# Projection weights split once: both parts kept in DRAM and reloaded as one piece for blocks 1 to 3

## The chip, the core and the metric

The kernel runs on one core of a Trainium2 chip. The metric is device microseconds of one execution. The engines named below are TensorE (matmuls; PE in the profile, its weight loads PEld), VectorE (DVE), ScalarE (ACT), GpSimd (POOL) and SyncE (SP), whose queue issues nearly all DMAs.

## The reference

A decoder layer over 2048 tokens of width 1024, all in float32:

```
h    = rmsnorm(x)
proj = h @ w_in                                   # 1024 x 3840
o    = concat(hgrn2(proj[:, :2048]), rwkv7(proj[:, 2048:]))     # two recurrences, 512 columns each
x    = x + o @ w_out                              # 1024 x 1024
x    = x + conv_ffn(rmsnorm(x))                   # up 1024 -> 2*2816, conv of width 3, SiLU gate, down
out  = rmsnorm(x)
```

## The kernel before

A product of two float32 matrices is made of three matmuls: each operand is split into a high part, its value in the type fp32r, and a low part, the rest. `mm3` (L286 to L288) multiplies high by high, high by low and low by high and sums them in PSUM. The split itself is a cast on ScalarE (L238 or L245) and a subtraction on VectorE (L239 or L246); `split` also takes the two buffers for the parts.

Phase 1 goes over four blocks of 512 tokens. `dense` is a list of jobs for TensorE: "A" transposes the normalized rows of a block into `hh` and `hl`, 30 jobs "P" multiply 128 columns of w_in each (8 steps of `mm3`, 24 matmuls), and "O", `out_block`, multiplies the finished output of the recurrences with w_out and adds x. An out_block has two halves of 256 tokens, `i2`; each half goes over two halves of the columns, `dh`, with 8 steps of k; each step loads one piece of w_out (128x512), splits it and multiplies it with two groups of 128 tokens, six matmuls. So the same 16 pieces of w_out are loaded and split twice per block. Jobs O of blocks 0 and 1 stand before the jobs of blocks 2 and 3, and that of block 2 at the end. Of w_in, `load` takes a job's weights as two halves of 128x4x128, and a job's load is called one job ahead (`load(i + 1)`), also across an O. The two recurrences (`rw_super`, `hg_unit`) advance in turn, and `fill` lets the dense jobs run between their stages for a fixed credit of estimated time (`TICK`).

Phase 2 begins with block 3's output projection (`o_operand`, `o_weights`), whose w_out pieces go through a ring of four raw slots, then comes the feed-forward part.

Instructions are not issued in the order of the code: the framework's scheduler simulates the kernel with costs of its own and a priority by program order, puts each engine's instructions in the order in which they start there, and gives out the buffers of a pool's tag as they come free. A tile waits for a free buffer of its tag. The tags here are "wraw" (4 buffers of 2 KB per partition, for raw weights, and also for x rows `xh` and the norms' scratch `nsq`), "wh" and "wl" (4 buffers each). The names with numbers below are tiles and their versions; `cst`, `gdt`, `g2`, `rw` and `yo` belong to the RWKV7 stream, `pj` is a PSUM bank of the dense jobs, `oT` is the recurrences' output in DRAM and `x1d` the residual there. ScalarE's functions come in sets, and changing the set is an instruction of its own, ACT_TABLE_LOAD: L114 where the code asks for it, L118 where it is put in ahead of an activation of another set.

Of the kernel before, what the change touches and what calls it, by code (L numbers as in the profile page):

```python
# [7 lines left out]
F32 = mybir.dt.float32  # L8
F32R = mybir.dt.float32r
# [9 lines left out]
P = 128  # L19
T = 2048  # L20
D = 1024
KD = D // P
# [38 lines left out]
def tile_layer(ctx, tc, consts, x, norm1_w, w_in, hg_lb_logits, hg_norm_w, rw_shift_mu, rw_w0, rw_w2,  # L61
# [3 lines left out]
    nc = tc.nc  # L65
    V, S, TE = nc.vector, nc.scalar, nc.tensor
    dma = nc.sync.dma_start

    cp = ctx.enter_context(tc.tile_pool(name="cp", bufs=1, reuse_waits="tile"))
    dp = ctx.enter_context(tc.tile_pool(name="dp", bufs=1, space=DRAM))  # L70
# [101 lines left out]
    KH = NFF // 2  # L172
    Sg = [[dp.tile([KH * P, BLK], F32, name=f"Sg{g}{i}") for i in range(4)] for g in range(2)]
    Tw = [dp.tile([KH * P, BLK], F32, name=f"Tw{i}") for i in range(4)]

    def krows(t_, q, kk):

        return t_[(q * KH + kk) * P:(q * KH + kk + 1) * P, :]
# [58 lines left out]
    def split_to(hi, lo, src):  # L237
        S.copy(hi, src)  # L238
        V.tensor_sub(lo, src, hi.bitcast(F32))  # L239

    def split(pool, src, shape, name, bufs):

        hi = pool.tile(shape, F32R, tag=name + "h", name=name + "h", bufs=bufs)
        lo = pool.tile(shape, F32R, tag=name + "l", name=name + "l", bufs=bufs)
        S.copy(hi, src)  # L245
        V.tensor_sub(lo, src, hi.bitcast(F32))  # L246
        return hi, lo
# [10 lines left out]
    def square_sum(junk, src, b, i, dh):  # L258

        q = 2 * ((b - 2) * 4 + i) + dh  # L260
        act(junk, src, AF.Square, accum_out=ssc[:, q:q + 1])
# [22 lines left out]
    def mm3(acc, lhs, rhs, first, last, skip=False):  # L284
        (lh, ll), (rh, rl) = lhs, rhs
        TE.matmul(acc, lh, rh, start=first, stop=False, skip_group_check=skip)  # L286
        TE.matmul(acc, lh, rl, start=False, stop=False, skip_group_check=skip)  # L287
        TE.matmul(acc, ll, rh, start=False, stop=last, skip_group_check=skip)  # L288

    def phase1(c1):  # L290
        hp = c1.enter_context(tc.tile_pool(name="hp", bufs=1, reuse_waits="tile"))
        wp = c1.enter_context(tc.tile_pool(name="wp", bufs=2, reuse_waits="tile"))
# [22 lines left out]
        def bank(kind):  # L315
            return ps.tile([P, 512], F32, tag=kind, name=kind, bufs=2)
# [79 lines left out]
        def out_block(nb, oh=None, ol=None):  # L396


            def half(t_, k):

                return t_[:, 4 + k // 2, (k % 2) * 256:(k % 2) * 256 + 256]

            for i2 in range(2):
                for dh in range(2):
                    accs = [bank("pj") for _ in range(2)]
                    for k in range(KD):
                        if i2 == 0 and dh == 0 and oh is None:
                            raw = wp.tile([P, BLK], F32, tag="wraw", name="oraw", bufs=4)
                            dma(raw, oT[nb][k * P:(k + 1) * P, :])
                            split_to(hh[:, k, :], hl[:, k, :], raw)  # L410
                        if i2 == 0 and dh == 1 and oh is not None:
                            raw = wp.tile([P, 256], F32, tag="wraw", name="oraw", bufs=4)
                            dma(raw, oT[nb][k * P:(k + 1) * P, 256:512])
                            split_to(half(hh, k), half(hl, k), raw)
                        raw = wp.tile([P, 512], F32, tag="wraw", name="woraw", bufs=4)
                        dma(raw, w_out[0, k * P:(k + 1) * P, dh * 512:dh * 512 + 512])
                        wh, wl = split(wp, raw, [P, 512], "w", 4)
                        if k == KD - 2:
                            xh = [wp.tile([P, 512], F32, tag="wraw", name="xh", bufs=4) for _ in range(2)]
                            for q in range(2):  # L420
                                t0 = nb * BLK + (i2 * 2 + q) * P
                                dma(xh[q], x[0, t0:t0 + P, dh * 512:dh * 512 + 512])
                        for q in range(2):
                            is_ = slice((i2 * 2 + q) * P, (i2 * 2 + q + 1) * P)
                            if oh is None:
                                lhs = hh[:, k, is_], hl[:, k, is_]
                            elif i2 == 0:
                                lhs = oh[k // 4][:, k % 4, is_], ol[k // 4][:, k % 4, is_]
                            else:
                                lhs = tuple(half(t_, k)[:, q * P:(q + 1) * P] for t_ in (hh, hl))  # L430
                            mm3(accs[q], lhs, (wh, wl), k == 0, k == KD - 1)
                            yield 680
                    for q in range(2):
                        V.tensor_add(xh[q], accs[q], xh[q])
                        r0 = (i2 * 2 + q) * P
                        if nb == 2:
                            square_sum(wp.tile([P, 512], BF16, tag="wraw", name="nsq", bufs=4), xh[q], 2,
                                       i2 * 2 + q, dh)
                        dma(x1d[nb][r0:r0 + P, dh * 512:dh * 512 + 512], xh[q])
# [51 lines left out]
        def dense():  # L491
# [39 lines left out]
            cols = [jb[1] for jb in jobs if jb[0] == "P"]  # L531
            loaded = {}

            def load(i):
                if i < len(cols) and i not in loaded:
                    ws = []
                    for k2 in range(2):
                        raw = wp.tile([P, 4, P], F32, tag="wraw", name="wraw", bufs=4)
                        dma(raw, w_in[0, k2 * 512:k2 * 512 + 512, cols[i]:cols[i] + P].rearrange("(k p) c -> p k c", p=P))
                        ws.append(split(wp, raw, [P, 4, P], "w", 4))  # L540
                    loaded[i] = ws

            i = 0
            load(0)
            for jb in jobs:
                if jb[0] == "E":
# [8 lines left out]
                if jb[0] in "OW":  # L555
                    while done["rw2"] < 2 * jb[1] + 2 or done["hg"] < 4 * jb[1] + 4:
                        yield None
                    if jb[0] == "W":
                        jb[2]()
                    else:  # L560
                        yield from out_block(jb[1], *(rows["O"] if jb[1] == 2 else ()))
                    continue
                _, col, ev, cond, fin = jb
                while not cond():
                    yield None
                load(i)
                ws = loaded.pop(i)
                load(i + 1)
                i += 1
                acc = bank("pj")  # L570
                for k in range(KD):
                    wh, wl = ws[k // 4]
# [491 lines left out]
    with ExitStack() as c2:  # L1064
# [6 lines left out]
        Bh, Bl = ([B_[f"{c}{i}"] for i in range(7)] for c in "hl")  # L1071
# [49 lines left out]
        for i, (lo_, hi_) in enumerate(((0, 88), (88, 176))):  # L1121
            vps = pst("cps")
            TE.transpose(vps[:, 0:88], crow[i], ident[0:88, 0:88])
            V.tensor_copy(cvt[:, lo_:hi_], vps[:, 0:88])
        rings = {"o": (Bh[2], []), "w": (Bl[2], [])}

        def ring(nm, src):

            t_, n_ = rings[nm]
            v = t_[:, len(n_) % 4, :]  # L1130
            n_.append(0)
            dma(v, src)
            return v
# [7 lines left out]
        def o_weights(k, dh):  # L1141

            wh, wl = (wr.tile([P, 512], F32R, tag="uraw", name="wo" + c, bufs=6) for c in "hl")
            split_to(wh, wl, ring("w", w_out[0, k * P:(k + 1) * P, dh * 512:dh * 512 + 512]))
            return wh, wl

        junk = uc.tile([P, 512], BF16, tag="c", name="nsq", bufs=6)
# [4 lines left out]
        for n, k in enumerate(ks):  # L1152
            op = o_operand(k)
            if n == 3:
                A0 = up_raw(0, A0_)
            if n in (4, 6):
                for i in range(4):
                    dma(xh_[2 * n - 8 + i], x[0, 3 * BLK + i * P:3 * BLK + (i + 1) * P, (n // 2 - 2) * BLK:(n // 2 - 1) * BLK])
            for dh in range(2):
                w = o_weights(k, dh)  # L1160
                for i in range(4):
                    is_ = slice(i * P, (i + 1) * P)
                    mm3(accs[dh][i], (op[0][:, is_], op[1][:, is_]), w, n == 0, n == KD - 1)
                if n == KD - 1:
                    for i in range(4):
                        xt = xh_[4 * dh + i]
                        V.tensor_add(xt, accs[dh][i], xt)
                        square_sum(junk, xt, 3, i, dh)
                        dma(x1d[3][i * P:(i + 1) * P, dh * BLK:(dh + 1) * BLK], xt)
            if n >= 2:  # L1170
                for q in range(2 * n - 4, 2 * n - 2):
                    build(0, (0, 1, 4)[q // 4], q % 4)
# [167 lines left out]
    with tc.tile_pool(name="dn", bufs=1, reuse_waits="tile") as dn:  # L1340
# [59 lines left out]
        for s_ in range(3, N):  # L1400
            g, p, kk = steps[s_]
# [53 lines left out]
```

## Time and profile before

| | |
|---|---|
| runs | 2796.88 us median of 3 (2792.88 to 2805.77) |
| profiled execution | 2796.34 us, span 2794.2 us |
| mean granted TensorE clock | 0.985 |
| HBM read / written | 325.94 MB / 105.91 MB |
| input projections of blocks 0, 1, 2, 3 | about 0-330, 330-560, 720-950, 1080-1330 us |
| output projections of blocks 0, 1, 2 | about 560-720, 950-1080, 1330-1450 us |
| phase 2 | from about 1450 us |

In the rows of stretches each engine stands with its busy time and its instructions, in the order PE, PEld, DVE, ACT, POOL, and then the granted clock (1.00 is full), the mean busy share of the 16 DMA queues and GB/s. In rows of groups "out<-in" are tile names, then partitions x elements and type, then the count, the busy us and mean ns of one, and the idle time of the engine ahead of them with what ended it.

### The profile page before, as it was taken

How to read it: one execution, taken by the hardware profiler on the slowest of the kernel's cores; microseconds unless marked ns; L12 is line 12 of the kernel's file. 1: busy time of each engine (PE TensorE's matmuls, PEld its weight loads, DVE VectorE, ACT ScalarE, POOL GpSimd, SP SyncE). 2: the span in 40 equal slices, each digit the busy share in tenths (PEclk: the TensorE clock that was granted, in tenths of full speed). 3: DMA queues.
4: the chain of work that ended last, by engine and by line, in shares of the span. 5: the costliest groups of instructions: out<-in, count | busy, mean ns of one | idle time of the engine just before them, and what ended most of it. 6: DMA issues, size and time to landing. Idle time of an engine off the chain costs nothing.

```text
span 2794.2 us, 47708 instructions
## 1 busy us (share of the span) xinstructions
PE 2681.3 (96%) x18059; PEld 2133.3 (76%) x18059; DVE 2061.9 (74%) x3875; ACT 1408.5 (50%) x2236; POOL 4.0 (0%) x10
## 2 busy tenths in 40 slices
PE   6999999989999989999889999999999999999998
PEld 5777778766787767777768887887888888777887
DVE  4877768694586855777748889978989877667656
ACT  4545454543645424735446555556555555445444
POOL 0000000000000000000000000000000000000000
PEclk9999999998999989999899999999999999999999
DMA  4222323244352345542357767525455423999865
GB/s 151 72 71 73 101 69 82 62 140 124 95 153 64 92 130 158 158 129 84 99 186 274 232 215 257 186 73 181 154 200 189 132 79 128 326 326 319 286 193 186
DMA packets 429204, 435.01 MB, mean 156 GB/s; under 512 B 68279, under 2 KB 287661, under 8 KB 428973
## 3 DMA queue, kind: packets, MB, share of 16 engines
q1 hardware_dynamic: 428077, 429.33, 48.3%
q8 instruction: 142, 2.33, 0.3%
q0 software_dynamic: 608, 2.10, 0.2%
q14 instruction: 89, 0.73, 0.1%
q10 hardware_dynamic: 288, 0.52, 0.0%
HBM read 325.94 MB, written 105.91 MB: 155 GB/s over the span
## 4 chain that ended last, share of the span: by engine, by line
PE 39%; DMA 5%; DVE 5%; issue 2%; ACT 1%; SPq 1%; DVEq 0%; ACTq 0%
PE ua L286 5%; PE ua L288 5%; PE ua L287 5%; PE ud L288 2%; PE ud L286 2%; PE ud L287 2%; PE db L287 2%; PE db L286 2%; PE db L288 2%; PE da L287 2%; PE da L288 1%; PE da L286 1%; PE ub L288 1%; PE ub L286 1%; PE ub L287 1%
## 5 line engine op out<-in xcount | busy, mean ns | idle before, releaser
L286 PE MATMUL pj<-hh,wh 128*128 128x512 f32 x960 | 400.9, 418 | 4.4 <-DVE hl L482 4.4
L287 PE MATMUL pj<-hl,wh 128*128 128x512 f32 x960 | 380.4, 396 | 0.0
L288 PE MATMUL pj<-hh,wl 128*128 128x512 f32 x960 | 379.2, 395 | 0.0
L245 ACT CAST wh<-wraw 128x512 fp32r<-128x512 f32 x240 | 147.3, 619 | 339.0 <-PE pj L287 273.6
L286 PE MATMUL ua<-Bh,uwh 128*128 128x512 f32 x704 | 276.3, 393 | 3.2 <-ACT m L118 3.2
L288 PE MATMUL ua<-Bh,uwl 128*128 128x512 f32 x704 | 274.5, 390 | 0.3 <-DVE uwl L246 0.3
L287 PE MATMUL ua<-Bl,uwh 128*128 128x512 f32 x704 | 274.0, 389 | 0.0
L246 DVE TENSOR_TENSOR wl<-wraw,wh 128x512 fp32r<-128x512 f32 x240 | 163.2, 684 | 130.7 <-ACT wh L245 127.8
L286 PEld LDWEIGHTS pj<-hh,wh 128*128 128x128 f32 x960 | 181.0, 188 | 57.9 <-issue 15.0
L287 PEld LDWEIGHTS pj<-hl,wh 128*128 128x128 f32 x960 | 181.1, 189 | 41.7 <-issue 7.8
L288 PEld LDWEIGHTS pj<-hh,wl 128*128 128x128 f32 x960 | 180.8, 188 | 40.2 <-issue 1.9
L245 ACT CAST uwh<-uraw 128x512 fp32r<-128x512 f32 x215 | 132.3, 617 | 133.8 <-PE ua L287 61.7
L245 ACT CAST dah<-draw 128x512 fp32r<-128x512 f32 x151 | 93.8, 621 | 185.4 <-DMA draw<-Sg 54.8
L246 DVE TENSOR_TENSOR dal<-draw,dah 128x512 fp32r<-128x512 f32 x151 | 104.0, 689 | 108.7 <-ACT dah L245 104.8
L246 DVE TENSOR_TENSOR uwl<-uraw,uwh 128x512 fp32r<-128x512 f32 x215 | 146.3, 684 | 44.6 <-ACT uwh L245 44.6
L286 PEld LDWEIGHTS ua<-Bh,uwh 128*128 128x128 f32 x704 | 132.2, 188 | 32.4 <-ACT m L118 5.3
L288 PEld LDWEIGHTS ua<-Bh,uwl 128*128 128x128 f32 x704 | 132.2, 188 | 29.4 <-DVE uwl L246 1.6
L287 PEld LDWEIGHTS ua<-Bl,uwh 128*128 128x128 f32 x704 | 132.3, 188 | 26.9
L288 PE MATMUL ud<-Bh,uwl 128*128 128x512 f32 x352 | 137.1, 390 | 0.6 <-DVE uwl L246 0.6
L286 PE MATMUL ud<-Bh,uwh 128*128 128x512 f32 x352 | 136.9, 389 | 0.0
L287 PE MATMUL ud<-Bl,uwh 128*128 128x512 f32 x352 | 136.9, 389 | 0.0
L287 PE MATMUL da<-dbl,dah 128*128 128x512 f32 x340 | 133.6, 393 | 1.4 <-DVE dbl L246 1.2
(313 smaller groups left out, 5940.5 us busy)
## 6 DMA issues: line engine op xcount, KB each, us to landing
wraw<-in_w_in_dram SPq DMA_DIRECT2D x240, 256.0 KB
uraw<-in_w_up_dram SPq DMA_DIRECT2D x172, 256.0 KB
woraw<-in_w_out_dram SPq DMA_DIRECT2D x96, 256.0 KB
draw<-Sg SPq DMA_DIRECT2D x88, 256.0 KB
draw<-Tw SPq DMA_DIRECT2D x88, 256.0 KB
gd<-y SPq DMA_DIRECT2D x86, 256.0 KB
xt<-x1d SPq DMA_DIRECT2D x32, 512.0 KB
draw<-gd SPq DMA_DIRECT2D x63, 256.0 KB
```

The costliest lines, as they stand in the source:

```text
L245: S.copy(hi, src)
L246: V.tensor_sub(lo, src, hi.bitcast(F32))
L286: TE.matmul(acc, lh, rh, start=first, stop=False, skip_group_check=skip)
L287: TE.matmul(acc, lh, rl, start=False, stop=False, skip_group_check=skip)
L288: TE.matmul(acc, ll, rh, start=False, stop=last, skip_group_check=skip)
```

## The change

For w_in, block 0's 30 jobs (60 halves) split as before, into one tile of 128x2x512 whose two planes are the high and the low part, and store that tile to a new DRAM tensor w_in_d, 512 KB at a time, from GpSimd's queue. The jobs of blocks 1 to 3 load these 512 KB into the tile and split nothing. For w_out the first half of block 0's out_block splits and stores its 16 pieces to w_out_d; all later halves (80 pieces) load both parts. In phase 2 `o_weights` loads the two parts into two tiles, without the ring and the split. Tags "wh" and "wl" are replaced by one tag "w", 4 buffers of both parts; "wraw" keeps its 4.

```diff
+    w_in_d = dp.tile([60, P, 2, 512], F32, name="w_in_d")
+    w_out_d = dp.tile([16, P, 2, 512], F32, name="w_out_d")
...
-                        raw = wp.tile([P, 512], F32, tag="wraw", name="woraw", bufs=4)
-                        dma(raw, w_out[0, k * P:(k + 1) * P, dh * 512:dh * 512 + 512])
-                        wh, wl = split(wp, raw, [P, 512], "w", 4)
+                        wt = wp.tile([P, 2, 512], F32R, tag="w", name="w", bufs=4)
+                        wh, wl = wt[:, 0], wt[:, 1]
+                        if nb == 0 and i2 == 0:
+                            raw = wp.tile([P, 512], F32, tag="wraw", name="woraw", bufs=4)
+                            dma(raw, w_out[0, k * P:(k + 1) * P, dh * 512:dh * 512 + 512])
+                            split_to(wh, wl, raw)
+                            nc.gpsimd.dma_start(w_out_d[dh * KD + k], wt.bitcast(F32))
+                        else:
+                            dma(wt.bitcast(F32), w_out_d[dh * KD + k])
...
-                        raw = wp.tile([P, 4, P], F32, tag="wraw", name="wraw", bufs=4)
-                        dma(raw, w_in[0, k2 * 512:k2 * 512 + 512, cols[i]:cols[i] + P].rearrange("(k p) c -> p k c", p=P))
-                        ws.append(split(wp, raw, [P, 4, P], "w", 4))
+                        wt = wp.tile([P, 2, 512], F32R, tag="w", name="w", bufs=4)
+                        n_ = 2 * (i % 30) + k2
+                        if i < 30:
+                            raw = wp.tile([P, 512], F32, tag="wraw", name="wraw", bufs=4)
+                            dma(raw.rearrange("p (k c) -> p k c", c=P),
+                                w_in[0, k2 * 512:k2 * 512 + 512, cols[i]:cols[i] + P].rearrange("(k p) c -> p k c", p=P))
+                            split_to(wt[:, 0], wt[:, 1], raw)
+                            nc.gpsimd.dma_start(w_in_d[n_], wt.bitcast(F32))
+                        else:
+                            dma(wt.bitcast(F32), w_in_d[n_])
+                        ws.append([wt[:, j].rearrange("p (k c) -> p k c", c=P) for j in range(2)])
...
-            split_to(wh, wl, ring("w", w_out[0, k * P:(k + 1) * P, dh * 512:dh * 512 + 512]))
+            for j, t_ in enumerate((wh, wl)):
+                dma(t_.bitcast(F32), w_out_d[dh * KD + k, :, j])
```

Counted in the two built programs: casts of these weights 352 before and 76 now, subtractions the same; 76 stores from GpSimd; table loads 57 and 83; matmuls alike, 13917.

The edit also changes the order. On TensorE, at the end of block 1's out_block, the RWKV7 stream's matmuls (L866, L878) stood among the steps of the projection before, with its last two and a half steps following L878:

```order
L866 MATMUL rw_10862<-yo_10841,cst_63 128x512 x2
L286 MATMUL pj_10757<-wh_10875,hh_187 128x512
L287 MATMUL pj_10757<-wl_10876,hh_187 128x512
L288 MATMUL pj_10757<-wh_10875,hl_188 128x512
L286 MATMUL pj_10758<-wh_10875,hh_187 128x512
L287 MATMUL pj_10758<-wl_10876,hh_187 128x512
L288 MATMUL pj_10758<-wh_10875,hl_188 128x512
L286 MATMUL pj_10757<-wh_10887,hh_187 128x512
L287 MATMUL pj_10757<-wl_10888,hh_187 128x512
L288 MATMUL pj_10757<-wh_10887,hl_188 128x512
L878 MATMUL rw_10894<-gdt_8443,g2_175 128x512 x2
```

Now (L878 is L895, L286 to L288 are L289 to L291, one tile `w` holds both parts) the last matmul of the stream comes earlier and ten steps, 60 matmuls, follow it without another; the first two of them:

```order
L895 MATMUL rw_10224<-gdt_8005,g2_177 128x512
L289 MATMUL pj_9935<-w_10052,hh_189 128x512
L290 MATMUL pj_9935<-w_10052,hh_189 128x512
L291 MATMUL pj_9935<-w_10052,hl_190 128x512
L289 MATMUL pj_9936<-w_10052,hh_189 128x512
L290 MATMUL pj_9936<-w_10052,hh_189 128x512
L291 MATMUL pj_9936<-w_10052,hl_190 128x512
L289 MATMUL pj_9935<-w_10082,hh_189 128x512
L290 MATMUL pj_9935<-w_10082,hh_189 128x512
L291 MATMUL pj_9935<-w_10082,hl_190 128x512
```

What moved are the stream's matmuls: out of the projection's last steps, to a place ahead of them. (At the end of block 0's out_block four such steps follow one another.)

On SyncE, at the same place, raw pieces were loaded with x rows and stores between them, the next job's w_in (L539) ahead of the last two stores:

```order
L416 DMA woraw<-in_w_out_dram 128x512 x3
L439 DMA x1d_126<-xh 128x512 x2
L416 DMA woraw<-in_w_out_dram 128x512 x5
L422 DMA xh<-in_x_dram 128x512 x2
L416 DMA woraw<-in_w_out_dram 128x512
L1002 DMA oT_123<-osq 128x512
L539 DMA wraw<-in_w_in_dram 128x4x128 x2
L881 DMA oT_123<-yo 128x2x512
L439 DMA x1d_126<-xh 128x512 x2
```

Now each load is of both parts (L426), into a buffer of "w", and the next job's w_in (L556) comes behind the last of them:

```order
L426 DMA w<-w_out_d 128x1024
L431 DMA xh<-in_x_dram 128x512
L426 DMA w<-w_out_d 128x1024 x5
L898 DMA oT_123<-yo 128x2x512
L448 DMA x1d_126<-xh 128x512 x2
L426 DMA w<-w_out_d 128x1024 x7
L556 DMA w<-w_in_d 128x1024 x2
L448 DMA x1d_126<-xh 128x512 x2
```

The loads stand seven in a row where raw loads stood five, with the last w_in pieces moved behind them. Two of the four buffers of "w" hold the next P job's weights while the out_block of block 0 or 1 runs, since that job's load is called before it; in block 2's no P job follows and all four serve it.

On ScalarE, early in block 2, the first norms (`nsq`, `nst`) stood some twenty instructions behind the block's transposes (`hh`), among weight casts and the evictions of P jobs (`rkv`), and ran on with two table loads:

```order
L245 CAST wh<-wraw 128x512
L118 ACTIVATE nsq,nst<-xt 128x1024 x2
L118 ACTIVATE rkv_7462<-pj,omu 128x512
L245 CAST wh<-wraw 128x512
L118 ACT_TABLE_LOAD
L118 ACTIVATE nst<-nst,eps_75 128x1
L118 ACTIVATE nsq,nst<-xt 128x1024
L118 ACT_TABLE_LOAD
L118 ACTIVATE ai<-rw,vt 128x512 x4
```

Now they follow the transposes at once, between the first evictions:

```order
L118 ACTIVATE hh<-pj,vt 128x512 x8
L118 ACTIVATE nsq,nst<-xt 128x1024 x2
L118 ACT_TABLE_LOAD
L118 ACTIVATE nst<-nst,eps_75 128x1
L118 ACTIVATE tl<-pj,omu 128x512
L118 ACT_TABLE_LOAD
L118 ACTIVATE nst<-nst 128x1
L118 ACTIVATE nsq,nst<-xt 128x1024
L118 ACTIVATE tl<-tl 64x512
L118 ACT_TABLE_LOAD
L118 ACTIVATE nst<-nst,eps_75 128x1
```

The norms moved ahead, and every switch between them and the evictions is a table load.

In phase 2 the first three pairs of w_out parts are issued on SyncE ahead of the last x1d stores of block 2's out_block; before, the raw pieces followed them.

More of the change, by code (lines that the diff above doesn't have):

```diff
@@ L1124, in tile_layer @@
             V.tensor_copy(cvt[:, lo_:hi_], vps[:, 0:88])
-        rings = {"o": (Bh[2], []), "w": (Bl[2], [])}
+        rings = {"o": (Bh[2], [])}
         def ring(nm, src):
```

## The prediction

> **What bounds the kernel now.** I read the page first, then stretches of the run, then the waits, and last single tiles and the chain.
>
> ```profile
> span 2794.2 us, 47708 instructions
> PE 2681.3 (96%) x18059; PEld 2133.3 (76%) x18059; DVE 2061.9 (74%) x3875; ACT 1408.5 (50%) x2236; POOL 4.0 (0%) x10
> L245 ACT CAST wh<-wraw 128x512 fp32r<-128x512 f32 x240 | 147.3, 619 | 339.0 <-PE pj L287 273.6
> L246 DVE TENSOR_TENSOR wl<-wraw,wh 128x512 fp32r<-128x512 f32 x240 | 163.2, 684 | 130.7 <-ACT wh L245 127.8
> ```
>
> TensorE is busy 96% of the span. A cast costs 619 ns on ScalarE and a subtraction 684 ns on VectorE, but ScalarE mostly waits for TensorE to give back a buffer (273.6 us): the weights are split ahead of need. So work removed there counts only where TensorE waits. Where that is, the run by stages tells; the columns are stretch and length, busy time of each engine (instructions), granted clock, DMA share, GB/s.
>
> ```profile
> 0.00:330.00 330.00, 299.33 (x2449) 234.41 (x2449) 235.79 (x552) 160.49 (x251) 0.20 (x4) 1.00 0.34 97
> 330.00:560.00 230.00, 227.52 (x2296) 174.89 (x2293) 161.88 (x358) 119.14 (x182) 0.00 (x0) 1.00 0.25 69
> 560.00:720.00 160.00, 145.78 (x1364) 110.33 (x1364) 104.89 (x243) 66.05 (x104) 0.00 (x0) 0.93 0.45 138
> 720.00:950.00 230.00, 224.99 (x1969) 176.55 (x1968) 166.69 (x370) 127.60 (x200) 0.00 (x0) 1.00 0.33 91
> 950.00:1080.00 130.00, 114.89 (x1093) 84.12 (x1092) 85.48 (x197) 53.07 (x86) 0.00 (x0) 0.91 0.46 140
> 1080.00:1330.00 250.00, 242.28 (x2042) 190.59 (x2041) 179.61 (x390) 130.33 (x197) 1.96 (x3) 1.00 0.42 126
> 1330.00:1450.00 120.00, 104.20 (x1059) 80.32 (x1057) 76.46 (x183) 47.53 (x89) 1.79 (x3) 0.90 0.41 125
> 1450.00:2794.00 1344.00, 1322.33 (x5802) 1082.14 (x5802) 1051.09 (x1587) 704.30 (x1128) 0.00 (x0) 1.00 0.62 208
> ```
>
> Rows 3, 5 and 7 are the output projections of blocks 0, 1 and 2: TensorE idles 14.2, 15.1 and 15.8 us there, and the clock averages 0.93, 0.91 and 0.90, worth another 11 to 12 us each. The input projections of blocks 1 to 3 (rows 2, 4, 6) idle 2.5, 5.0 and 7.7 us. That is the whole pool from which lighter vector work can gain. The change decides in the three output projections, and there it also removes buffering.
>
> **The change part by part.** Removed: 180 + 80 + 16 = 276 casts and subtractions, 171 us of ScalarE and 189 us of VectorE. Against TensorE's idle time it is worth far less. In the second output projection VectorE is the late one:
>
> ```profile
> 950.00:975.00 25.00, 22.84 (x159) 18.46 (x158) 24.29 (x66) 13.10 (x23) 0.00 (x0) 1.00 0.37 109
> 975.00:1000.00 25.00, 18.84 (x172) 12.04 (x172) 21.72 (x59) 4.97 (x9) 0.00 (x0) 0.79 0.68 191
> 1350.00:1375.00 25.00, 19.30 (x188) 14.49 (x186) 20.39 (x59) 5.27 (x11) 0.54 (x1) 0.73 0.51 138
> 975.00:1000.00 25.00, 3.41 (x5) 3.09 (x5) 0.79 0.68 191
> 600.00:625.00 25.00, 6.53 (x10) 5.59 (x9) 1.00 0.63 195
> ```
>
> The last two rows are the work on the w_out tiles alone (VectorE, ScalarE). Of TensorE's 6.2 idle us in 975:1000, at most VectorE's 3.4 us on weights can come back, and some of what stands before it: I take 4 us, 7 us for block 2's projection (5.7 idle in 1350:1375, and the loop of weight loads below), and a third of the 15.2 us in rows 2, 4, 6, since only a part of those waits is behind a cast: 5. Sum -16, between 0 and -46 (all idle of rows 2, 4, 5, 6, 7).
>
> Added: one buffer now holds both parts, four of them; during the output projections of blocks 0 and 1 the next input projection's two prefetched halves hold two of the four. Before, these two slots were fed by four raw tiles that were loaded ahead. Now the load itself waits until TensorE has given the slot back: no slack is left but one step of six matmuls. Its price is a round trip.
>
> ```profile
> 2000.00:2100.00 100.00, 100.00 (x443) 82.84 (x442) 91.07 (x131) 51.75 (x74) 0.00 (x0) 1.00 0.57 191
> L416 SPq DMA_DIRECT2D woraw<-in_w_out_dram x96: 327/328/1250, 567.9 to 1439.8; - x96
> 1420.33 3.19 DMA woraw<-in_w_out_dram
> 1427.62 4.52 DMA woraw<-in_w_out_dram
> 1638.69 6.11 DMA xt<-x1d
> xt<-x1d SPq DMA_DIRECT2D x32, 512.0 KB
> oT<-osq POOLq DMA_DIRECT2D x4, 256.0 KB, 3.8
> oT<-yo POOLq DMA_DIRECT2D x2, 512.0 KB, 4.0
> ```
>
> A full TensorE starts a matmul every 100 / 443 = 0.226 us, so a step is 1.35 us. A load is issued in 0.33 us; 256 KB land in 3.2 to 4.5 us, 512 KB in 4.0 to 6.1, and from 256 to 512 KB the two rows of POOL's queue differ by 0.2. I take 4.2 us, just above the lower end since the projection runs at a DMA share near 0.46: 4.5 us from release to use. Two steps then take 1.35 + 4.5 = 5.85 us instead of 2.70. In block 1's projection the built order now ends with ten steps back to back: five pairs at 3.15 us lost, 15.8 us. The other 22 have other matmuls between; in 600:625 the kernel before made ten steps in 25 us, 5.0 a pair, later seven to nine, 5.6 to 7.1 a pair, so they lose little: 2 us. Term +18 (11 with a landing of 3.2, 36 and more with 6.1). In block 0's projection the second half reads whole pieces; its last four steps stand bare, two pairs, 6.3 us: +6 (4 to 14).
>
> By the Trainium skill, DMA: Bandwidth & Descriptors, Anatomy of one DMA, a GpSimd transfer takes 2.0 us plus its bytes over 436 GB/s, an estimate of 3.2 us for 512 KB; the trace has 4.0 on that queue, so the measurement decides. With 3.2 the term of 18 would be the 11 given as its lower end.
>
> The first half of block 0's projection still splits, and its slot is now also held until the store has landed: cast 0.62, subtraction 0.68, store 4.0, 5.3 us for two steps and the hand-overs against 5.0 now: +4 (0 to 12). The same stores in block 0's input projection have two further buffers and a job of 24 x 0.226 = 5.4 us for cover; 31 MB over 330 us put 95 GB/s on queues at a share of 0.34: +1 (0 to 5). Input projections of blocks 1 to 3 load two pieces per job into four buffers, 4.5 us behind 5.4 us of matmuls: 0, and were that cover gone, 1 us a job.
>
> Moved: with the raw tiles free, the norms' square sums and roots are placed earlier, among other functions of ScalarE; 26 more table loads stand in the built order (83 instead of 57), all of the kind that L118 does.
>
> ```profile
> L118 ACT ACT_TABLE_LOAD x8 | 10.3, 1283 | 0.1
> 744.00:768.00 24.00, 21.56 (x89) 14.99 (x89) 19.38 (x26) 23.77 (x37) 0.00 (x0) 1.00 0.08 22
> 744.58 1.28 ACT L118 ACT_TABLE_LOAD   x1
> ...
> 762.19 1.28 ACT L118 ACT_TABLE_LOAD   x1
> ```
>
> That is 26 x 1.283 = 33 us of ScalarE, which is busy 50% and gives back more than that (171). Four of the present eight lie between the last two rows, and there, with ScalarE full, TensorE idles 24.00 - 21.56 = 2.4 us, 0.6 per load: 26 x 0.6 = 16 at the worst, 0 if a matmul queue covers each. Most of the new ones fall between weight casts that are gone; I take +4.
>
> The junction to phase 2 loads both parts of 16 w_out pieces instead of the raw one: 16 x 256 KB = 4.2 MB more.
>
> ```profile
> 1450.83 4.16 DMA Bl<-in_w_out_dram
> 1475.00:1480.00 5.00, 5.00 (x24) 4.14 (x23) 3.36 (x6) 2.41 (x6) 0.00 (x0) 1.00 1.04 390
> 1490.00:1495.00 5.00, 5.00 (x24) 4.14 (x23) 3.95 (x7) 3.41 (x7) 0.00 (x0) 1.00 0.60 178
> ```
>
> At 390 GB/s, with the queues full in the second row, that is 10.8 us of transfer; behind it the DMA share falls to 0.60 while TensorE never stopped, so the loads run ahead and a few us later the queues catch up. The first piece needs no cast any more (0.62), and its 4.16 us is less exposed as three pairs are issued ahead of block 2's last stores. I take +1, between -2 (that cast and a part of the first landing) and +11 (no cover).
>
> The clock. The bare pairs leave TensorE 2.7 of 5.85 us busy, 46%.
>
> ```profile
> 624.00:626.00 2.00, 0.93 (x18) 0.58 (x16) 1.84 (x6) 0.00 (x0) 0.00 (x0) 1.00 0.78 204
> 626.00:628.00 2.00, 1.31 (x20) 0.96 (x20) 2.00 (x7) 0.62 (x1) 0.00 (x0) 0.94 0.46 70
> 628.00:630.00 2.00, 2.00 (x33) 1.38 (x32) 1.47 (x4) 0.00 (x0) 0.00 (x0) 0.50 0.43 66
> 626.69 0.66 PE L928 MATMUL hg<-hX 128*64 128x32 f32 x16 [1.74 <-DVE hX L907]
> ```
>
> Over the first two of these rows TensorE is busy 2.24 of 4 us, 56%, and then it is granted 0.50, which no single gap over 1.74 us preceded. At half clock only the second step of a pair lies on the path in full (the first overlaps the round trip), 1.35 us a pair: 5 x 1.35 = 6.8, of which I take 4 (0 to 10: block 0's pairs with them).
>
> The Trainium skill, TensorE: Matmul & The Clock Gate, What's actually happening, puts half clock after at least one idle window of about 3.4 us; the gap of 1.74 us ahead of the 0.50 row does not bear a window of pure idleness out, and if that rule decided, the waits of 3.15 us would not lower the clock: the clock term would be 0 and the sum 4 less.
>
> **Sum.** -16 + 18 + 6 + 4 + 1 + 0 + 4 + 1 + 4 = +22. The profiled execution took 2796.34 us (2794.2 of span and 2.1 around it), within 0.02% of the median 2796.88, so no correction: 2818. What this kernel's measurement can tell from no change is about 0.5%, 14 us: from 2783 to 2811 is "same".
>
> **Rivals.** *Faster.* The output projections wait for a landed and split tile, and both go away. The waits of the split are the largest single ones on that stream:
>
> ```profile
> ACT wh L245 <- DMA woraw<-in_w_out_dram: 53.1, 30, 4.7
> PEld pj L286 <- ACT wh L245: 11.9, 12, 2.7
> ```
>
> ScalarE lost 53.1 us on landings, TensorE 11.9 us on the split. If release to use is 3.5 us or less (landing 3.2), a pair is 4.85 us, no worse than the present 5.0, and the two-slot terms fall from 24 to about 10; if then the projections no longer sink below full clock, 3 x 11 us of clock loss come back by half. Sum: -16 + 11 + 4 + 1 + 1 + 3 + 1 + 0 - 17 = -12, and with a relief of 21 instead of 16: 2779. It decides from a landing at or below 3.5 us and needs the clock besides; against it stands 4.52 us beside 3.19 in the same projection, for half the bytes. Chance 0.20.
>
> *No change.* The round trip is short but the clock stays as it is: -16 + 11 + 4 + 1 + 1 + 2 + 1 = +4, with a little more relief 0: 2797 to 2801. For it speaks that TensorE loses only 15 us per projection in all, so anything that moves inside can stay small. 0.24.
>
> *Much slower.* 512 KB land like the 6.11 row: a pair takes 1.35 + 6.11 + 0.33 = 7.8 us, five bare pairs lose 25, and the other 22 steps, 11 pairs of 5.6 on average, lose some 2 each, 22 more; half of it in block 0 with 14, and half clock 10: -16 + 47 + 14 + 4 + 1 + 4 + 1 + 7 = +62: 2858. Against it: 4.0 on POOL's queue for as many bytes, and a DMA share of only 0.46 here. 0.12.
>
> **How the numbers follow.** My forecast has the remaining 0.44, with 2811 to 2838 as its own range (landing from 3.9 to 4.9 us). Faster by over 14 us needs the first rival: 0.20. Within: 0.24. Slower: 0.44 + 0.12 = 0.56. The range leaves out a part of the dear rival and a tail below the relief's: 2775 to 2852.
>
> **What the profile after would show.** In block 1's output projection the weight loads are issued only after a matmul on the same slot, TensorE waits for DMA about 3 us in every second step at its end, and the stretch grows by about 18 us; block 0's by about 10; block 2's, which has all four buffers, shrinks by about 7. The casts count 76 instead of 352 on these weights, the table loads 83. The input projections of blocks 1 to 3 keep their length within 3 us each. I am wrong if the pairs at the end run at 3 us each (loads issued earlier than I read from the order), if TensorE waits for SyncE's queue behind a store in these stages, or if phase 2 changes by more than 5 us.

## The result: 1.35% slower, and the profile after

The changed kernel takes 2833.49 us (median of 4 runs, 2830.24 to 2835.66) against 2795.84 of the kernel before on the same chip: ratio 1.0135, interval 1.0113 to 1.0157. The forecast was 2818, the range 2775 to 2852.

The page of the changed kernel; then, from the groups, the table loads that are put in ahead of activations; then two waits of SyncE's queue (us in total, times, longest), and after them the first of the two as it was in the kernel before:

```profile
span 2832.0 us, 47097 instructions
PE 2693.6 (95%) x18059; PEld 2143.9 (76%) x18059; DVE 1905.0 (67%) x3599; ACT 1296.0 (46%) x1986; POOL 44.9 (2%) x86
```

```profile
L118 ACT ACT_TABLE_LOAD x34 | 43.6, 1283 | 0.6
```

```profile
SPq L556 <- PE pj L291: 581.2, 161, 22.8
SPq L426 <- PE pj L291: 130.2, 66, 7.9
```

```profile
SPq L539 <- DVE wl L246: 422.5, 131, 13.0
```

VectorE lost 157 us of work and ScalarE 113, and still the span grew by 37.8. TensorE's busy time grew by 12.3 us (2693.6 against 2681.3) with the same matmuls: that is clock (the mean granted one is 0.979, before 0.985). Its idle time grew by 25.5 (138.4 against 112.9). A weight load now waits in SyncE's queue for a matmul (L291) to give its buffer back; before, it waited for a subtraction (L246).

The stretches of the changed kernel, in the columns explained for the kernel before: the halves of block 0's and then block 1's output projection, block 3's input projection, block 2's output projection. The two rows behind them are the halves of block 1's output projection in the kernel before.

```profile
595.50:661.70 66.20, 54.44 (x407) 36.41 (x406) 48.10 (x127) 21.56 (x37) 8.01 (x15) 0.85 0.79 258
661.70:725.40 63.70, 53.33 (x585) 37.48 (x583) 18.02 (x33) 15.68 (x22) 0.00 (x0) 0.95 0.58 187
982.30:1052.50 70.20, 59.11 (x779) 45.53 (x779) 39.17 (x107) 16.16 (x27) 0.00 (x0) 0.95 0.59 183
1052.50:1109.20 56.70, 42.01 (x224) 27.50 (x223) 13.68 (x21) 11.29 (x14) 0.00 (x0) 0.90 0.62 204
1109.20:1373.60 264.40, 259.07 (x2129) 205.42 (x2130) 159.06 (x365) 111.40 (x151) 1.84 (x3) 0.97 0.57 183
1373.60:1479.80 106.20, 91.77 (x972) 70.47 (x970) 47.89 (x122) 28.28 (x56) 1.80 (x3) 0.91 0.70 231
```

```profile
961.80:1032.60 70.80, 60.52 (x730) 45.39 (x728) 47.01 (x116) 25.25 (x43) 0.00 (x0) 0.83 0.41 119
1032.60:1080.60 48.00, 42.90 (x274) 29.08 (x273) 27.25 (x49) 22.92 (x34) 0.00 (x0) 1.00 0.57 181
```

Cut at the same matmuls in both traces, the stages compare as follows (us; "phase 2" runs from the first matmul of block 3's output projection to the last of the kernel). The right column gives the same stage over all the profiled kernels below that do the stage in the changed way, since one execution of the same code differs from another by some us in a stage.

| stage | before | after | changed way, all |
|---|---|---|---|
| input projections of blocks 0, 1, 2, 3 | 269.6, 285.8, 257.5, 260.6 | 271.3, 292.3, 256.9, 264.4 | means of 9: 270.8, 294.7, 258.1, 263.8 |
| output projection, block 0 | 116.8 | 129.9 | 125.2 to 132.3 (7) |
| block 1 | 118.8 | 126.9 | 123.9 to 129.4 (7) |
| block 2 | 114.4 | 106.2 | 106.2 to 111.0 (11) |
| phase 2 | 1330.7 | 1344.4 | 1344.4 to 1346.3 (3) |

In the two profiled executions the span differs by 37.8 us, and the stages make 38 of it: block 0's and 1's output projections +21, phase 2 +14, the input projections +11, block 2's output projection -8.

**The two-buffer wait, seen.** Of the chain of waits through the second half of block 1's output projection (start, us), the landings, and the two links ahead of the load that starts at 1076.01; then the waits of TensorE there; then the stretch of its ten steps without other matmuls between them:

```profile
1054.18 6.04 DMA w<-w_out_d
1069.64 3.35 DMA w<-w_out_d
1074.73 0.70 DVE xh L443
1075.45 0.47 SPq L448
1076.01 5.89 DMA w<-w_out_d
1084.91 3.22 DMA w<-w_out_d
1089.86 3.14 DMA w<-w_out_d
1094.74 3.22 DMA w<-w_out_d
```

```profile
PE pj L289 <- DMA w<-w_out_d: 11.0, 10, 4.7
```

```profile
1070.70:1099.70 29.00, 18.68 (x60) 12.18 (x60) 4.53 (x5) 0.26 (x1) 0.00 (x0) 0.88 0.63 209
```

From 1084.91 to 1094.74 two pairs of steps take 4.9 us each, of which 3.2 are the landing. The two landings near 6 us stand beside stores (`x1d` from 1052.62, `oT` and `x1d` from 1073.61), and the load at 1076.01 was also issued late, behind an x1d store (L448) that waited for VectorE. All ten steps took 29.0 us, 5.8 a pair; TensorE idled 10.3 us of them.

### The profile page after: what moved, and what is told of

It is laid out like the page before. It is cut to its first block, busy times and chain, and to the rows that moved or that the text cites. A ratio compares the mean times of both kernels' runs of the same rounds, so it can differ in the third digit from the quotient of the medians.

```text
span 2832.0 us, 47097 instructions
## 1 busy us (share of the span) xinstructions
PE 2693.6 (95%) x18059; PEld 2143.9 (76%) x18059; DVE 1905.0 (67%) x3599; ACT 1296.0 (46%) x1986; POOL 44.9 (2%) x86
## 4 chain that ended last, share of the span: by engine, by line
PE 67%; DMA 10%; issue 8%; DVE 7%; ACT 5%; SPq 2%; POOL 0%; DVEq 0%; ACTq 0%; POOLq 0%
PE pj L289 7%; PE pj L291 7%; PE pj L290 7%; PE ua L289 5%; PE ua L291 5%; PE ua L290 5%; DMA w<-w_out_d 2%; PE ud L291 2%; PE ud L290 2%; PE ud L289 2%; PE da L290 2%; PE da L289 2%; PE da L291 2%; DMA sraw<-gd 1%; PE db L289 1%
## 5 line engine op out<-in xcount | busy, mean ns | idle before, releaser
L289 PE MATMUL pj<-hh,w 128*128 128x512 f32 x960 | 406.5, 423 | 5.4 <-DVE hl L491 3.4
L290 PE MATMUL pj<-hl,w 128*128 128x512 f32 x960 | 380.6, 396 | 0.0
L291 PE MATMUL pj<-hh,w 128*128 128x512 f32 x960 | 380.1, 396 | 0.0
L289 PE MATMUL ua<-Bh,uwh 128*128 128x512 f32 x704 | 277.4, 394 | 13.0 <-ACT uwh L248 9.5
L291 PE MATMUL ua<-Bh,uwl 128*128 128x512 f32 x704 | 275.1, 391 | 0.0
L289 PEld LDWEIGHTS pj<-hh,w 128*128 128x128 f32 x960 | 182.8, 190 | 60.3 <-issue 14.1
L290 PEld LDWEIGHTS pj<-hl,w 128*128 128x128 f32 x960 | 183.0, 191 | 42.5 <-issue 9.2
L291 PEld LDWEIGHTS pj<-hh,w 128*128 128x128 f32 x960 | 182.5, 190 | 40.0
L289 PEld LDWEIGHTS ua<-Bh,uwh 128*128 128x128 f32 x704 | 132.7, 188 | 42.4 <-ACT uwh L248 9.9
L291 PEld LDWEIGHTS ua<-Bh,uwl 128*128 128x128 f32 x704 | 132.7, 188 | 28.9 <-DVE uwl L249 1.0
L291 PE MATMUL ud<-Bh,uwl 128*128 128x512 f32 x352 | 137.0, 389 | 0.0
L289 PE MATMUL ud<-Bh,uwh 128*128 128x512 f32 x352 | 136.9, 389 | 0.0
L291 PE MATMUL da<-dbh,dal 128*128 128x512 f32 x340 | 132.4, 390 | 0.0
L289 PE MATMUL da<-dbh,dah 128*128 128x512 f32 x340 | 127.9, 390 | 2.1 <-ACT dbh L248 2.1
```

## Experiments

**e3: all four buffers for the projection.** After an out_block the next P job's weights are loaded, not before it:

```diff
-                load(i + 1)
+                if next((q[0] for q in jobs[ji + 1:] if q[0] in "PO"), None) == "P":
+                    load(i + 1)
...
                         yield from out_block(...)
+                        load(i)
```

> As the changed kernel, but the P job that follows an out_block is loaded behind that out_block in program order, so that all four buffers of w serve the projection. Theory (two buffers alone make each pair of steps wait for a landing): the second half of block 1's projection falls from 56.7 to about 46 us, block 0's second half from 63.7 to about 57, its first half from 66.2 to about 62: 2812 to 2819 us, and the next P job does not wait, since its load runs under the transposes. Rival (the projections are longer because the recurrences' matmuls now come earlier and leave bare steps, whatever the buffers): 2829 to 2834 us, with over 10 us of TensorE idle still in block 1's second half.

Measured: 2807.56 us, ratio 1.0038 (1.0024 to 1.0052): 26 us of the 37.7 are back. The first half of block 0's, then the halves of block 1's output projection:

```profile
598.30:649.40 51.10, 38.92 (x224) 27.43 (x223) 41.16 (x108) 14.90 (x25) 7.78 (x14) 0.85 0.88 300
974.90:1042.70 67.80, 60.16 (x742) 48.50 (x741) 37.98 (x104) 14.58 (x25) 0.00 (x0) 0.82 0.58 181
1042.70:1087.30 44.60, 40.13 (x262) 27.58 (x261) 15.40 (x27) 13.25 (x17) 0.00 (x0) 1.00 0.85 276
```

In block 1's second half TensorE's idle time fell from 14.7 to 4.5 us and the stretch from 56.7 to 44.6. Block 0's second half became longer (68.7, where the theory had 57) and its first shorter; the sum, 119.9, is 10 below the changed kernel. The gain is above the range of the theory. TensorE's wait for landings in block 1's second half is nearly gone, 0.5 us instead of 11.0:

```profile
PE pj L289 <- DMA w<-w_out_d: 0.5, 1, 0.5
```

The time and the idle time that the rival named did not come. But e3 changed the order together with the buffers: counted in the traces, block 1's projection ends with 15 matmuls without another between them in e3, as in the kernel before, and with 60 in the changed kernel. So e3 takes away the held buffers and the bare steps at once, and does not separate them. The changed kernel's own trace helps. In block 2's projection, which all four buffers serve, three bare steps (18 of the row's 22 matmuls) took 4.7 us, 3.1 a pair against the 5.8 with two buffers, and in that whole projection TensorE waited 0.4 us for a landing:

```profile
1384.20:1388.90 4.70, 4.70 (x22) 3.66 (x21) 3.99 (x12) 1.32 (x2) 0.12 (x1) 1.00 0.83 268
```

```profile
PE pj L289 <- DMA w<-w_out_d: 0.4, 1, 0.4
```

A long bare run with four buffers stands in no run here, so how the 26 us divide between buffers and order stays open.

**e1, e2, e10, e12: the start of phase 2.** e1 puts `split_to(wh, wl, ring("w", w_out[...]))` back in `o_weights`. e2 loads the parts from GpSimd's queue (`nc.gpsimd.dma_start`). e10 takes the high parts from the ring: `wh = t_[:, len(n_) % 4, :].bitcast(F32R)`. e12 issues `x1d[3]` from GpSimd's queue.

> Phase 2's o_weights goes back to the raw piece through the ring of four slots and the split; all else as in the changed kernel. Theory (three pairs of buffers hold both parts, their loads wait on SyncE's queue for TensorE, and the h2d loads stand behind them): from the start of block 3's output projection to the first up products the changed kernel lost 4.7 + 9.1 = 13.8 us, and these come back: 2818 to 2822 us, the single wait of 9.5 us ahead of the first ua products gone. Rival (the loss there is carried in from phase 1, whose last block writes and reads more): 2829 to 2834 us, the wait still there.

> As the changed kernel, but the 32 loads of w_out parts in phase 2 are issued from GpSimd's queue instead of SyncE's: same bytes, same three pairs of buffers. Theory (what hurts is that the h2d loads stand in SyncE's queue behind loads that wait for a buffer): the 9.5 us wait goes, 2820 to 2825 us. Rival (the 4.2 MB more are what hurts, by filling the DMA queues): 2830 to 2835 us, the h2d loads as late as now.

> As the changed kernel, but the high parts of o_weights in phase 2 go into the ring of four that the raw pieces had, the low parts into the six buffers as before: four or more pairs instead of three, same bytes, same queue. Theory (three pairs make SyncE wait, and the h2d loads behind it): the idle time from block 3's projection to the end falls from 22 to about 14 us, 2822 to 2829 us. Rival (the bytes): 2831 to 2836 us, the wait of 9.5 us ahead of the first ua products still there.

> As the changed kernel, but block 3's eight x1d stores in phase 2, which wait for the last sums of its output projection, are issued from GpSimd's queue; the w_out parts are loaded as in the changed kernel, same bytes, three pairs, SyncE's queue. Theory (the 9.5 us wait comes from the order in SyncE's queue: w_out loads that wait push twelve Ts loads and the first w_up loads behind those stores): the wait ahead of the first ua products falls below 3 us, 2822 to 2828 us. Rival (4.2 MB more fill the queues, so that the same loads land late wherever they stand): the wait stays above 6 us, 2830 to 2835 us.

Measured: e1 2820.94, ratio 1.0091 (1.0072 to 1.0110), 12.5 us back; e2 2833.27 (1.0115 to 1.0145); e10 2829.03 (1.0089 to 1.0135); e12 2835.69 (1.0118 to 1.0153). TensorE's waits at the first `ua` products, of the changed kernel and of e1, e2, e10 and e12, in this order:

```profile
PE ua L289 <- ACT uwh L248: 9.5, 1, 9.5
```

```profile
PE ua L289 <- ACT uwh L248: 0.7, 1, 0.7
```

```profile
PE ua L289 <- ACT m L118: 1.9, 1, 1.9
PE wacc L290 <- DMA wol<-w_out_d: 2.8, 5, 1.0
```

```profile
PE ua L289 <- ACT uwh L248: 9.6, 1, 9.6
```

```profile
PE ua L289 <- ACT m L118: 4.3, 1, 4.3
```

And SyncE's queue (start, us from the first issue to the last, count), first of the kernel before, then of the changed one:

```profile
1484.32 12.02 SPq L1076 DMA_DIRECT2D br<-Ts  x10
1497.79 0.32 SPq L1169 DMA_DIRECT2D x1d<-xh  x1
...
1509.67 3.71 SPq L1109 DMA_DIRECT2D uraw<-in_w_up_dram  x6
```

```profile
1527.26 2.11 SPq L1187 DMA_DIRECT2D x1d<-xh  x4
1529.65 2.11 SPq L1187 DMA_DIRECT2D x1d<-y  x4
1531.86 9.82 SPq L1093 DMA_DIRECT2D br<-Ts  x12
...
1546.85 11.81 SPq L1126 DMA_DIRECT2D uraw<-in_w_up_dram  x7
```

Before, ten Ts loads went out ahead of the stores that wait for the last sums of block 3; now twelve go out behind them, and the first w_up loads behind those. The chain that ended the 9.5 us wait runs through one of these Ts loads (from 1539.76, 4.33 us), the load of x1d rows behind them (from 1545.85, 5.01 us) and two activations of 1.15 us ahead of the cast. The cause is the w_out loads (e1, within the range of its theory). The other three show parts of it in the trace: another queue takes the 9.5 us wait away and leaves 1.9 for an eviction (e2), but lengthens block 3's projection by small waits on landings (52.1 us instead of 50.4); four pairs instead of three take the waits out of the projection (46.2 us) and leave 9.6 (e10); moving the stores leaves a wait of 4.3, for an eviction too (e12). Phase 2 takes 1338.6 to 1338.8 us in all three, 6 less than in the changed kernel, against 1326.0 in e1. So order and buffers are worth about 6 us in each; the three were not run together. In the time none of the three is clear: the intervals of e2 and e12 hold the changed kernel's ratio, and e10's reaches it. e2's time is that of its rival, while its wait went as its theory said; e10's time is at the upper end of its theory, while its wait stayed as its rival said. Phase 1, the same code in all five kernels, took from 1479.8 to 1494.1 us in the profiled executions, which hides 6 us. e12 met neither number of its two theories. The other 8 to 13 us that e1 gives back in phase 2 (which took 1330.7 in the kernel before) stay with loading both parts; whether as 4.2 MB more or as loads on the path was not separated.

**e5, e6, e8, e7, e11: the parts of the change alone.** e5 keeps only the w_in part. e6 keeps only the w_out part of phase 1. e8 is e6 with the edit of e3. e7 is the changed kernel with the edits of e1 and e3. e11 is e8 with block 0 split in both halves and stored in the second:

```diff
-                        if nb == 0 and i2 == 0:
+                        if nb == 0:
...
-                            nc.gpsimd.dma_start(w_out_d[dh * KD + k], wt.bitcast(F32))
+                            if i2 == 1:
+                                nc.gpsimd.dma_start(w_out_d[dh * KD + k], wt.bitcast(F32))
```

> Only the w_in part of the change: w_out is split at each use as before, phase 2's o_weights too; the weights' tile of both parts and its four buffers stay. Theory (loss = 11 us in the input projections + 13.5 in the output projections + 13.8 at the start of phase 2, each by its own cause): block 1's input projection stays near 293 us, the output projections and phase 2 are as before: 2804 to 2810 us. Rival (the input projections suffer from the w_out loads and stores, or the table loads come from both): 2796 to 2801 us.

> Only the w_out part of phase 1: w_in is split in every block as before, and o_weights of phase 2 stays with the raw ring. Its built program has the 57 table loads of the kernel before. Theory: input projections as before (block 1's near 286 us at full clock), block 0's and 1's output projections longer by 13 and 9 us, block 2's shorter by 8: 2806 to 2812 us. Rival (split w_in tiles hold their buffers longer, so the projections lose less, or the load of the raw pieces runs ahead as before): 2793 to 2800 us.

> The changed kernel with both cures: the next P job's weights are not held through an out_block, and o_weights has its raw ring back. Theory (the causes are separate, -26 and -12.5 us by their own runs): 2833 - 38 = 2795, 2792 to 2798 us. Rival (they overlap, both being about what SyncE's queue brings late): 2800 to 2806 us.

> Only the w_out part in phase 1, with the next P job's weights not held through an out_block. Theory (input projections as before, all four buffers for the projections): block 2's projection shorter by 7, block 1's by 6, block 0's about +3: 2784 to 2790 us, faster than the kernel before. Rival (with w_in split, the projection's gain is eaten by the next job's split behind it and by half clock): 2794 to 2800 us.

> The w_out part in phase 1 alone, without weights held through an out_block, and block 0 as before in both halves, with the parts stored in the second half, so that only blocks 1 and 2 load them. Theory (block 0 loses by stores and by short-lived reloads, blocks 1 and 2 gain 7 and 5): block 0's output projection falls from 119.9 to about 117 us, 2784 to 2789 us. Rival (the store in the second half holds four buffers as it did in the first): 2788 to 2793 us.

| kernel | us | ratio (interval) |
|---|---|---|
| e5, w_in alone | 2801.64 | 1.0014 (1.0002 to 1.0026) |
| e6, w_out alone | 2811.85 | 1.0054 (1.0039 to 1.0069) |
| e7, both cures | 2797.87 | 0.9999 (0.9988 to 1.0010) |
| e8, w_out alone, four buffers | 2789.11 | 0.9971 (0.9958 to 0.9983) |
| e11, the same for blocks 1 and 2 only | 2784.57 | 0.9949 (0.9929 to 0.9968) |

e6, e7, e8 and e11 lie within the ranges of their theories. The parts add up: 5.5 + 15.7 by medians and 12.5 for phase 2 make 33.7 of 37.7. e5 fell between the ranges of its theory and its rival: its input projections are as long as expected (block 1's 292.6 us), but block 0's output projection was 112.0, 4.8 shorter than before. With both cures the changed kernel is no slower than the kernel before, and no faster: what the w_out part gains with four buffers (e8, 7.0 us), the w_in part loses (e5, 5.5). e11 is faster than both; its block 0's projection takes 119.3, not 117, and it has 56.0 of that in the first half, where e8 had 67.0.

```profile
span 2782.8 us, 47496 instructions
PE 2675.1 (96%) x18059; PEld 2137.4 (77%) x18059; DVE 2023.8 (73%) x3811; ACT 1371.8 (49%) x2172; POOL 12.5 (0%) x26
```

Against the kernel before, 6.2 us of TensorE's busy time are gone (clock) and 5.2 of its idle time.

**e4 and e9: what the input projections lose.** Block 1's is the worst, 294.7 us in the mean of the nine kernels with w_in from DRAM; with w_in split, in e6, e8 and e11, it takes 287.6 to 288.1. In the changed kernel TensorE waits there twice behind the burst of table loads, and near 485 us the clock falls:

```profile
PE pj L289 <- ACT rkv L118: 2.1, 1, 2.1
PE rw L783 <- DMA TZ<-Td: 1.6, 1, 1.6
```

```profile
480.02:483.43 3.41, 2.22 (x74) 1.95 (x72) 2.77 (x9) 1.35 (x3) 0.00 (x0) 1.00 0.77 262
483.44:490.27 6.83, 6.74 (x76) 4.55 (x78) 0.77 (x2) 2.42 (x5) 0.00 (x0) 0.50 0.01 3
```

```profile
482.67 0.24 PE L797 MATMUL rw<-TTs,TZ 32*32 32x32 f32 x2 [0.68 <-ACT TZ L118]
483.53 1.09 PE L987 MATMUL hg<-cst,hk 128*128 128x128 f32 x4 [0.61 <-DVE hk L980]
```

e4 ties every activation with a table to the load that the code asked for:

```diff
-        if pre is not None:
-            tc.add_manual_dep(i_.ins, pre.ins.name, NOSYNC, reason="table order")
+        if want is not None:
+            tc.add_manual_dep(i_.ins, tab["pre"].ins.name, NOSYNC, reason="table order")
```

> As the changed kernel, but every activation with a table of its own is ordered behind the table load that the code asked for, so that the norms' roots cannot run ahead among other functions: 49 table loads instead of 83. Theory (the bursts of table loads hold up evictions and with them TensorE): block 1's input projection falls from 292.3 to about 287 us, 2825 to 2830 us in all. Rival (the loads are hidden; block 1's 6.5 us come from late loads on SyncE's queue): 2831 to 2835 us, that stretch still 291 to 293.

Measured: 2843.53 us, ratio 1.0174 (1.0158 to 1.0190): 10 us slower than the changed kernel, outside both; block 1's input projection took 297.1 us, where the theory had 287. Its page:

```profile
span 2841.0 us, 47064 instructions
PE 2703.5 (95%) x18059; PEld 2155.3 (76%) x18059; DVE 1904.0 (67%) x3599; ACT 1250.9 (44%) x1952; POOL 44.8 (2%) x86
```

TensorE idles 137.5 us, as in the changed kernel (138.4), and is busy 9.9 us longer: the whole loss is clock. Near 490 us it now stays low for longer:

```profile
485.00:490.00 5.00, 3.95 (x142) 3.69 (x138) 4.08 (x12) 2.39 (x5) 0.00 (x0) 0.83 0.37 112
490.00:495.00 5.00, 5.00 (x25) 3.11 (x22) 0.23 (x1) 1.18 (x2) 0.00 (x0) 0.50 0.01 3
```

So taking 34 table loads away, with the order that comes of it, wins nothing. e9, on the base of e5, loads and splits the raw half again beside the parts, in place and unused:

```diff
+                            raw = wp.tile([P, 512], F32, tag="wraw", name="wraw", bufs=4)
+                            dma(raw.rearrange("p (k c) -> p k c", c=P), w_in[...])
+                            S.copy(raw.bitcast(F32R), raw)
+                            V.tensor_sub(raw, raw, raw)
                             dma(wt.bitcast(F32), w_in_d[n_])
```

> Only the w_in part of the change, with the work that it removed put back beside it: in blocks 1 to 3 the raw half is loaded too, cast and subtracted in place, and not used; the matmuls read the parts from DRAM. In its built order block 1 has no longer the stretch of 76 small matmuls in a row at its fifth sixth of dense work, which stands in the w_in part alone. Theory (block 1's loss comes from the order that lighter ScalarE and VectorE bring: the stream's small matmuls clump, leave gaps and draw half clock): block 1's input projection falls from 292.6 to 286 to 289 us, no half clock near 485 us; all in all 2796 to 2801 us. Rival (the parts arrive late, since their loads wait for TensorE in SyncE's queue): 292 us or more there, with still more to load, 2803 to 2810 us.

Measured: 2838.17 us, ratio 1.0142 (1.0116 to 1.0167), 36 above e5. From 480 to 490 us, first e9, then e5:

```profile
480.00:490.00 10.00, 9.64 (x97) 7.74 (x96) 9.72 (x32) 0.69 (x1) 0.00 (x0) 1.00 0.66 188
```

```profile
480.00:490.00 10.00, 8.71 (x128) 6.48 (x124) 2.68 (x8) 3.79 (x7) 0.00 (x0) 0.68 0.10 39
```

As its order said, the clump of small matmuls and the half clock near 485 us are gone; but the input projections of blocks 1, 2 and 3 take 297.9, 272.8 and 279.7 us, with new waits of the streams. Its theory had 2796 to 2801 us; the rival had 292 us or more for block 1, which came, but no more than 2810 in all. Block 1 has a stretch at half clock elsewhere: from 422.2 to 429.0 us the clock is 0.50 in e9 and 1.00 in e5. So the half clock near 485 us goes with the clump, and the same work, put where it no longer holds a weight, costs 32 us in blocks 2 and 3; what makes block 1's stretch 7 us longer stays open.

## Why the prediction came out as it did

The direction and the range held; the sum of +22 stands against 37.7, with terms wrong on both sides. That the range held is in part luck. Without the clock's +4, the terms add up by stage to +14 for block 1's output projection (+8.1 came), +10 for block 0's (+13.1), -7 for block 2's (-8.2), 0 for the input projections (+11.4) and +1 for phase 2 (+13.7): what was too dear in the first hid a part of what was missing in the last two.

- *Two buffers in block 1's projection, +18:* the waits are in the trace, and they go when the weights are not held (e3), but the size was wrong: with the -4 of relief it was +14, and the stage grew by 8.1, in the seven kernels by 5 to 11. The step that failed is the landing of 4.2 us. It was 3.1 to 3.4 where no store stood beside the load, a pair then takes 4.9 us, and the 11 given as the lower end was the right value: TensorE waited 11.0 us for landings and idled 10.4 us more in the stage than before (25.8 against 15.4). The 22 other steps showed no loss in the first half, where 16 of them stand (70.2 us against 70.8, with a better clock). The Trainium skill, DMA: Bandwidth & Descriptors, Anatomy of one DMA, gives its formula for transfers on GpSimd's path; by it 512 KB were 3.2 us, an estimate. SyncE's loads agree with that here, and GpSimd's own stores do not (4.0 us before, 4.5 now); so the row of the stores was the wrong one for these loads.
- *Block 0's projection, +6 and +4:* +13.1, in the seven kernels +8 to +16. Right in sign and order.
- *Relief, -16:* block 2's -7 came as -8.2, in the eleven kernels -3 to -8; block 1's -4 shows only where no weights are held, in e3, e7, e8 and e11, whose projection takes 111.4 to 113.7 against 118.8. The -5 in the input projections did not come: TensorE's idle time did fall in blocks 2 and 3 (3.3 against 5.0, 5.3 against 7.4), but block 3 gave it back in clock (0.97 against 1.00) and block 1 lost 6.5.
- *P jobs 0, table loads +4:* the loads do hold TensorE up twice, by 3.7 us together, but without them nothing is gained (e4). The step that failed is to price 26 loads one by one, without the order that comes with them; e4 and e9 point at where the streams' small matmuls then stand, but do not prove it. That P jobs lose nothing failed with it: with w_in from DRAM the four input projections take 987.4 us together in the mean of the nine kernels, against 973.5 before and 974 to 980 in e6, e8 and e11, and the cause of most of that stays open.
- *Junction, +1, -2 to +11:* it cost 12.5 by e1; about 6 of it show as order and buffers in the profiled phase 2. The step that failed is "the loads run ahead", read from a DMA share in a trace whose loads had four raw buffers of their own; with three pairs the queue waits, and what is behind it slides past the stores. That loads behind a waiting load on SyncE are late too was priced nowhere in the sum.
- *Clock, +4, 0 to 10:* TensorE's busy time says 12.3, and mostly elsewhere: +5.1 in block 0's output projection, +5.9 in block 3's input projection, -2.3 in block 1's output projection, for which most of the term was meant. The bare steps there did draw half clock (0.88 over 29.0 us), but the first half of that projection was better off than before (0.95 against 0.83). The step that failed is to add the new loss of clock without asking what of the old one goes. A part of the new half clock stands in runs of small matmuls with short gaps: near 485 us TensorE was busy 2.22 of 3.41 us, with gaps of 0.68 and 0.61 us, and then got 0.50 for 6.8 us. The rule that the prediction weighed, from the Trainium skill, TensorE: Matmul & The Clock Gate, What's actually happening, half clock after at least one idle window of about 3.4 us, would have made this term 0; there is no such window in these rows. The Trainium skill, TensorE: Matmul & The Clock Gate, A second HAM failure mode: psum-queue depth-cycling, tells of a kernel that cycled through PSUM banks, in which TensorE idled briefly between groups of matmuls often enough for the gate to oscillate. The rows agree with that.

Of the three signs of being wrong that it named, the pairs at 3 us each did not come (4.9 and more). The other two did: one load at the end of block 1's projection stood in SyncE's queue behind a store (at 1076.01), and phase 2 changed by 13.7 us instead of at most 5. The input projections of blocks 1 and 3 grew by 6.5 and 3.8 us, where it had 3 at most.

The rival "faster" had its first condition met, landings of 3.2 us (but for the two near 6), and still did not come: of the 17 us of clock in its sum none came, since TensorE's busy time rose, and the losses in phase 2 and in the input projections were not in it.

## What to carry to other kernels

Before a split is traded for a load, count the buffers that the load can run ahead into, including those that a prefetch already holds: splitting had given the weights two stages of buffers and the load has one. On an in-order queue a load that waits for a late buffer delays every load behind it, and may drop them behind a store that waits for the end of the stage. An edit that changes the order can change the clock: the same matmuls kept TensorE busy for 2675.1 us in e11 and 2703.5 in e4. So compare TensorE's busy time for the same matmuls, not only its idle time.

## What the runs showed of the hardware

Half clock without any long idle: within a run of small matmuls TensorE was busy 2.22 of 3.41 us, with gaps of 0.68 and 0.61 us, and was then granted 0.50 for 6.8 us, in which it was busy for 6.7. In e4 the same matmuls took 9.9 us more of TensorE's time with its idle time unchanged, and all of its runs were granted less, 0.971 to 0.973 on average against 0.978 to 0.981. A load of 512 KB on SyncE's queue landed in 3.1 to 3.4 us, but in 5.9 and 6.0 us where stores were issued beside it.
